# Products with v in runs of four in the second attention, and ten tiles of probabilities

## The chip, the cores and the metric

The kernel runs on one core of a Trainium2 chip. The metric is the device time of one execution in microseconds. The core has five engines with a program each, which wait for each other through semaphores: TensorE (PE in the profile, its weight loads PEld), VectorE (DVE), ScalarE (ACT), GpSimd (POOL) and SyncE (SP), which issues most DMAs here.

## The reference

Two transformer blocks on 1024 tokens of width 1024, one after the other. The first has a sliding-window attention and an MLP. The second has low-rank attention with 8 heads, a Fourier branch, a gated merge of the two, and 16 experts that pick their tokens. The change lies in the second block's attention, over 1024 latent keys and 256 context keys:

```
q, k, v = _mla_qkv(p, ...)            # q, k: 8 heads of 96; v: 8 heads of 64
qc, kc, vc = _mla_qkv(pc, ...)
k_all = concatenate([k_lat, k_ctx])   # 1280 keys
s = einsum('bqhd,bkhd->bhqk', q, k) * 96 ** -0.5
o = einsum('bhqk,bkhd->bqhd', softmax(s), v)
x = x + g1 * _merge(p, o, fourier, ...)   # then the experts
```

## The kernel before, in words

The kernel is written against a tile layer: pools of named tiles with a number of buffers each, and a scheduler that puts every engine's instructions into one fixed order when the program is built. It goes by priority (the place in the code, unless `high_priority` lifts it) and by when it reckons operands and buffers to be ready. So the code's order is not the order on the engines: an instruction that is ready early moves up into another's gap.

`attend` (L1233) goes through the 8 heads in four pairs (`main`, L1255). In a pair it takes the 10 blocks of 128 keys (`j`), and for each the two halves of 512 queries (`half`); one such (j, half) is a step, 20 in a pair. In a step, for each of the two heads (`s`):

- three fp32r passes on TensorE give the scores with keys as rows, in a PSUM bank `st` (two banks), each operand being split into a high and a low part (L1278 to L1280);
- ScalarE takes the exponential into a tile `pt` in SBUF (L1282); the negated row maximum rides along as a 97th row of the operands, so no separate subtraction is needed. `pt` has `ATT_PT` buffers, 8 before;
- the sums for the denominator are added up elementwise in `acc` (L1290, L1292), on GpSimd for the key blocks 3, 6 and 8, else on VectorE.

The products with v follow one step later: `late` holds the step, and `weigh` (L1261) issues two matmuls (L1264), one a head, in plain fp32. Each uses 64 of TensorE's columns, because a head of v is 64 wide: head 0 writes partitions 0 to 63 of the bank `av[half]`, head 1 the others. They sum over the ten key blocks; after the tenth, ScalarE copies `av` out (L1267). `finish` (L1245) sums `acc` over partitions with a matmul of ones, also 64 columns a head, takes the reciprocal on VectorE (L1251) and scales (L1253). For a pair it is issued within the next one.

Beside the steps, two pieces at a time, goes the preparation of the next pair (`att_prep`, `aside` in the code): transposes of k and q into banks `tr` (L1176), copies out of them (L1179, L1180), and the row maxima: for each head and 128 queries, score matmuls into banks `mx` (two, L1203), which VectorE reduces (L1205). In the last pair `merge_ready` takes its place and splits operands for the merge; after the last pair come merge matmuls into banks named `st`, `mx` and `mg` (`mm3`, L132 to L134), of which those with `moh` and `mol` (the halves of the last pair's result) need the last two `finish`.

PSUM has 8 banks: tr 2, mx 2, av 2, st 2.

Of the kernel before, what the change touches and what calls it, by code (L numbers as in the profile page):

```python
# [33 lines left out]
MOE_LAST = 0  # L34
MOE_FIRST = 0, 1, 2, 3
ATT_FIN = (0, 1), (1, 0)
ATT_PT, ATT_GP, ATT_ACC, ATT_TR = 8, (3, 6, 8), 1, 2
MOE_SA = 0
TOP_GROUPS = (0, 1, 2, 3), (4, 5), (6,), (7,)
POWER = (0, 2, 3)  # L40
# [75 lines left out]
class Kern:  # L116
# [1116 lines left out]
    def attend(self, pools, p, ps, O, hd, got):  # L1233


        nc = self.nc
        tr = lambda: ps.tile([128, 512], F32, name="tr", bufs=ATT_TR)
        mx = bank = None
        if ATT_TR == 1:
            mx = lambda: ps.tile([128, 1536], F32, name="mx", bufs=1)  # L1240
        else:
            bank = lambda: ps.tile([128, 512], F32, name="mx", bufs=4 - ATT_TR)
        acc = {}

        def finish(hp, half):  # L1245
            tp = tr()
            for s in range(2):
                nc.tensor.matmul(tp[s * 64:s * 64 + 64, :], lhsT=self.ones[:, :64], rhs=acc[hp, half, s], start=True, stop=True,
                                 skip_group_check=True)
            R = p.tile([128, 512], F32, name="R", bufs=2)  # L1250
            nc.vector.reciprocal(R, tp)  # L1251
            o = O[hp][:, half * 512:half * 512 + 512]
            nc.vector.tensor_mul(o, o, R)  # L1253

        def main(hp, aside):  # L1255
            heads = [hd.pop(2 * hp + s) for s in range(2)]
            av = [ps.tile([128, 512], F32, name="av", bufs=2) for _ in range(2)]
            first = {}
            late = []

            def weigh():  # L1261
                j, half, pts = late.pop(0)
                for s in range(2):
                    nc.tensor.matmul(av[half][s * 64:s * 64 + 64, :], lhsT=self.v[j][:, 2 * hp + s, :], rhs=pts[s],  # L1264
                                     start=j == 0, stop=j == 9, skip_group_check=True)
                if j == 9:
                    nc.scalar.copy(O[hp][:, half * 512:half * 512 + 512], av[half])  # L1267

            for j in range(10):
                for half in range(2):  # L1270
                    sl = slice(half * 512, half * 512 + 512)
                    pts = []
                    for s in range(2):
                        qt, kt = heads[s]
                        st = ps.tile([128, 512], F32, name="st", bufs=2)
                        ks = slice(j * 128, j * 128 + 128)
                        mm = nc.tensor.matmul
                        mm(st, lhsT=kt[0][:, ks], rhs=qt[0][:, sl], start=True, stop=False)  # L1278
                        mm(st, lhsT=kt[0][:96, ks], rhs=qt[1][:96, sl], start=False, stop=False)
                        mm(st, lhsT=kt[1][:96, ks], rhs=qt[0][:96, sl], start=False, stop=True)  # L1280
                        pt = p.tile([128, 512], F32, name="pt", bufs=ATT_PT)
                        nc.scalar.activation(pt, st, AF.Exp)  # L1282
                        pts.append(pt)
                        if j == 0:
                            first[half, s] = pt
                        else:
                            eng = nc.gpsimd if j in ATT_GP else nc.vector
                            if j == 1:
                                acc[hp, half, s] = p.tile([128, 512], F32, name=f"acc{half}{s}", bufs=ATT_ACC)
                                eng.tensor_add(acc[hp, half, s], first[half, s], pt)  # L1290
                            else:
                                eng.tensor_add(acc[hp, half, s], acc[hp, half, s], pt)  # L1292
                    late.append((j, half, pts))
                    if len(late) > 1:
                        weigh()
                    if hp and (j, half) in ATT_FIN:
                        finish(hp - 1, ATT_FIN.index((j, half)))
                    next(aside, None)
                    next(aside, None)
            weigh()  # L1300
            for _ in aside:
                pass

        for hp in range(4):
            main(hp, self.att_prep(hp + 1, pools[(hp + 1) % 2], p, hd, tr, mx, bank) if hp < 3 else
                 self.merge_ready(pools[0], O, got))

        finish(3, 0)
        for half, name in ((0, "st"), (1, "mx")):
            sl = slice(half * 512, half * 512 + 512)  # L1310
            for m in range(2):
                pt = got["pt"][m, half] = ps.tile([128, 512], F32, name=name, bufs=2)
                for k in range(3):
                    self.mm3(pt, [x[:, k, :] for x in got["w"][m]], [x[:, sl] for x in got["o"][k]], k == 0, False)
            if half == 0:
                finish(3, 1)
# [784 lines left out]
```

## Time and profile before

| | |
|---|---|
| median of 3 runs | 2281.03 us (2279.44 to 2283.23) |
| the profiled execution | 2279.89 us |
| its span, first to last instruction | 2278.1 us |
| TensorE busy, mean granted clock | 2166.4 us (95%), 0.98 |
| VectorE, ScalarE, GpSimd busy | 1775.9, 1081.7, 565.2 us |
| the second attention, first st pass to end of the last pair | 1471.5 to 1767.2 us of the span |

The busy time of TensorE is made of modelled ends: a matmul's row gives its start exactly, its duration roughly. Matmuls overlap, so the difference of two starts tells what a matmul costs in the stream. In the timeline equal instructions that follow each other are one row with a count; a fp32 matmul shows as two records (two passes), a fp32r matmul as one.

### The profile page before, as it was taken

The numbers are of one execution on the slowest core, as the hardware profiler recorded it, in microseconds if no ns is written. First come the engines' busy times: TensorE is split into PE (matmuls) and PEld (weight loads), VectorE is DVE, ScalarE is ACT, GpSimd is POOL, SyncE is SP. The second block draws the span as 40 slices with busy tenths as digits, with TensorE's granted clock in tenths as the row PEclk, the third lists the DMA queues.
The fourth block names the chain that finished last, engine by engine and source line by source line (L and its number), as shares of the span: only waits on it lengthen the run. The fifth ranks groups of instructions, "written<-read, shape, count | busy, mean of one in ns | idle before, by whom it ended". The sixth has DMA issues, their size and how long they took to land. (4 is left out here: it accounts for less than half of the span.)

```text
span 2278.1 us, 29149 instructions
## 1 busy us (share of the span) xinstructions
PE 2166.4 (95%) x9954; PEld 1628.3 (71%) x9954; DVE 1775.9 (78%) x3047; ACT 1081.7 (47%) x1976; POOL 565.2 (25%) x489
## 2 busy tenths in 40 slices
PE   8999997999998999997999999999999998599997
PEld 7667685777776888875888988744444776488886
DVE  5777888898778889999444488776775678899997
ACT  5656555333333444464443375234335243278775
POOL 2111304222122113347121025121122422421121
PEclk9999998999999999999999999999999999699999
DMA  4000223556555432202333141300000865499995
GB/s 152 28 20 11 111 92 122 176 185 214 210 182 198 148 133 81 83 38 74 118 109 114 61 170 47 137 1 10 10 1 10 305 225 199 156 377 386 385 386 153
DMA packets 94965, 319.87 MB, mean 140 GB/s; under 512 B 13568, under 2 KB 15424, under 8 KB 94816
## 3 DMA queue, kind: packets, MB, share of 16 engines
q1 hardware_dynamic: 89856, 300.10, 36.0%
q0 software_dynamic: 4816, 17.39, 3.0%
q8 instruction: 78, 1.28, 0.2%
q14 instruction: 71, 0.58, 0.1%
q10 hardware_dynamic: 144, 0.52, 0.1%
HBM read 259.13 MB, written 58.75 MB: 140 GB/s over the span
## 5 line engine op out<-in xcount | busy, mean ns | idle before, releaser
L127 ACT CAST we_hi<-we_raw 128x1024 fp32r<-128x1024 f32 x192 | 200.1, 1051 | 60.5 <-PE gu L134 40.9
L128 DVE TENSOR_TENSOR we_lo<-we_raw,we_hi 128x1024 fp32r<-128x1024 f32 x188 | 222.1, 1222 | 3.7 <-ACT we_hi L127 3.4
L127 ACT CAST wup_h<-raw 128x512 fp32r<-128x512 f32 x154 | 94.9, 621 | 245.6 <-PE A L133 136.4
L128 DVE TENSOR_TENSOR wup_l<-raw,wup_h 128x512 fp32r<-128x512 f32 x154 | 122.6, 804 | 87.0 <-ACT wup_h L127 84.4
L1282 ACT ACTIVATE pt<-st 128x512 f32<-128x512 f32 x160 | 95.2, 596 | 134.9 <-PE st L1280 123.7
L132 PE MATMUL A<-uh,wup_h 128*128 128x512 f32 x364 | 146.9, 404 | 4.1 <-ACT a_raw L528 2.1
L133 PE MATMUL A<-ul,wup_h 128*128 128x512 f32 x364 | 146.2, 402 | 3.5 <-DVE ul L128 3.4
L134 PE MATMUL A<-uh,wup_l 128*128 128x512 f32 x364 | 145.2, 400 | 2.4 <-DVE wup_l L128 2.3
L127 ACT CAST dah<-a_raw 128x512 fp32r<-128x512 f32 x92 | 57.4, 623 | 139.5 <-PE B L133 67.5
L1264 PE MATMUL av<-pt,v 128*64 128x512 f32 x320 | 119.5, 616 | 0.0
L1292 POOL TENSOR_TENSOR acc<-acc,pt 128x512 f32<-128x512 f32 x48 | 65.3, 1375 | 211.8 <-ACT pt L1282 115.7
L441 POOL TENSOR_TENSOR wup_s<-raw 128x512 f32<-128x512 f32 x24 | 33.7, 1403 | 332.1 <-DVE raw L440 330.2
L1205 DVE TENSOR_REDUCE nm<-mx 128x1 f32<-128x512 f32 (+1 forms) x120 | 79.9, 687 | 43.9 <-PE mx L1203 42.8
L133 PE MATMUL B<-dwl,dah 128*128 128x512 f32 x272 | 107.5, 395 | 2.7 <-DVE dwl L128 2.6
L132 PE MATMUL B<-dwh,dah 128*128 128x512 f32 x272 | 107.2, 397 | 1.7 <-ACT dwh L127 1.7
L134 PE MATMUL B<-dwh,dal 128*128 128x512 f32 x272 | 106.8, 393 | 0.3 <-DVE dal L128 0.3
L133 PE MATMUL A<-dwl,dah 128*128 128x512 f32 x256 | 102.3, 400 | 4.4 <-DVE dwl L128 4.4
L132 PE MATMUL gu<-we_hi,xh 128*128 128x512 f32 x256 | 105.0, 410 | 0.0
L455 POOL TENSOR_TENSOR a_raw<-a_raw,a_raw 128x512 f32<-128x512 f32 x16 | 52.0, 3252 | 211.4 <-DVE a_raw L440 194.5
L132 PE MATMUL A<-dwh,dah 128*128 128x512 f32 x256 | 101.2, 398 | 2.7 <-ACT x_sq L812 2.7
L133 PE MATMUL gu<-we_lo,xh 128*128 128x512 f32 x256 | 102.0, 399 | 0.0
L134 PE MATMUL gu<-we_hi,xl 128*128 128x512 f32 x256 | 101.5, 396 | 0.0
(692 smaller groups left out, 6448.9 us busy)
## 6 DMA issues: line engine op xcount, KB each, us to landing
we_raw<-in_w_eg SPq DMA_DIRECT2D x64, 512.0 KB
we_raw<-in_w_eu SPq DMA_DIRECT2D x64, 512.0 KB
we_raw<-in_w_ed SPq DMA_DIRECT2D x64, 512.0 KB
h<-in_w_mod SPq DMA_DIRECT2D x48, 512.0 KB
raw<-in_w_up SPq DMA_DIRECT2D x32, 512.0 KB
ad<-r_out SPq DMA_DIRECT2D x32, 512.0 KB
a_raw<-ad SPq DMA_DIRECT2D x32, 512.0 KB
w_raw<-in_w_dn SPq DMA_DIRECT2D x32, 512.0 KB
```

What stands on the lines that cost most here:

```text
L127: pin(self.nc.scalar.copy(hi, raw))
L128: pin((eng or self.nc.vector).tensor_sub(lo, raw, hi.bitcast(F32)))
L132: mm(ps, lhsT=l[0], rhs=r[0], start=start, stop=False, **kw)
L133: mm(ps, lhsT=l[0], rhs=r[1], start=False, stop=False, **kw)
L134: mm(ps, lhsT=l[1], rhs=r[0], start=False, stop=stop, **kw)
L441: e[1].tensor_sub(t, x[3], x[0])
L455: e[3].tensor_add(x[2], x[2], x[3])
L1205: most = lambda o, i: nc.vector.tensor_reduce(o, i, axis=AX.X, op=OP.max, negate=True)
L1264: nc.tensor.matmul(av[half][s * 64:s * 64 + 64, :], lhsT=self.v[j][:, 2 * hp + s, :], rhs=pts[s], start=j == 0, stop=j == 9, skip_group_ch ...
L1282: nc.scalar.activation(pt, st, AF.Exp)
L1292: eng.tensor_add(acc[hp, half, s], acc[hp, half, s], pt)
```

## The change

`weigh` is called when two steps are held, ahead of the third, and issues the four products of both steps in a row. All but the first of the four have high priority and are kept in program order, which binds them to the first in the scheduler's order. The copies out follow the whole run. `ATT_PT` goes from 8 to 10.

```diff
-ATT_PT, ATT_GP, ATT_ACC, ATT_TR = 8, (3, 6, 8), 1, 2
+ATT_PT, ATT_GP, ATT_ACC, ATT_TR = 10, (3, 6, 8), 1, 2
...
+            def weigh():
+
+                ends = []
+                for n, (j, half, pts) in enumerate(late):
+                    for s in range(2):
+                        with self.tc.high_priority() if n + s else ExitStack():
+                            mm = nc.tensor.matmul(av[half][s * 64:s * 64 + 64, :], lhsT=self.v[j][:, 2 * hp + s, :], rhs=pts[s],
+                                                  start=j == 0, stop=j == 9, skip_group_check=True)
+                            if n + s:
+                                self.tc.keep_in_program_order(mm)
+                    if j == 9:
+                        ends.append(half)
+                late.clear()
+                for half in ends:
+                    nc.scalar.copy(O[hp][:, half * 512:half * 512 + 512], av[half])
+
             late = []
-
-            def weigh():
-                j, half, pts = late.pop(0)
-                for s in range(2):
-                    nc.tensor.matmul(av[half][s * 64:s * 64 + 64, :], lhsT=self.v[j][:, 2 * hp + s, :], rhs=pts[s],
-                                     start=j == 0, stop=j == 9, skip_group_check=True)
-                if j == 9:
-                    nc.scalar.copy(O[hp][:, half * 512:half * 512 + 512], av[half])
-
...
+                    if len(late) == 2:
+                        weigh()
                     late.append((j, half, pts))
-                    if len(late) > 1:
-                        weigh()
```

What it makes of the order on the engines, at three places. First TensorE in the first pair, key block 3 (`v_11879`), before:

```order
L1264 MATMUL av<-pt,v_11879 64x512
L1203 MATMUL mx<-kth,qth 128x512 x2
L1264 MATMUL av<-pt,v_11879 64x512
L1278 MATMUL st<-qth,kth 128x512
L1279 MATMUL st<-qtl,kth 128x512
L1280 MATMUL st<-qth,ktl 128x512
L1203 MATMUL mx<-kth,qth 128x512
L1278 MATMUL st<-qth,kth 128x512
L1279 MATMUL st<-qtl,kth 128x512
L1203 MATMUL mx<-kth,qth 128x256 x2
L1280 MATMUL st<-qth,ktl 128x512
L1264 MATMUL av<-pt,v_11879 64x512
```

and the same key block after (st is at L1286 to L1288 there, av at L1266):

```order
L1203 MATMUL mx<-kth,qth 128x512
L1286 MATMUL st<-qth,kth 128x512
L1287 MATMUL st<-qtl,kth 128x512
L1203 MATMUL mx<-kth,qth 128x512
L1288 MATMUL st<-qth,ktl 128x512
L1266 MATMUL av<-pt,v_11879 64x512 x4
L1203 MATMUL mx<-kth,qth 128x512
L1203 MATMUL mx<-kth,qth 128x256 x2
```

Before, mx matmuls stand between the two heads of a step; after, the four products of the key block follow each other.

Second, TensorE at the end of the last pair (`v_11884` is key block 8, the merge matmul of L133 writes an mx bank), before:

```order
L1278 MATMUL st<-qth,kth 128x512
L1279 MATMUL st<-qtl,kth 128x512
L1280 MATMUL st<-qth,ktl 128x512
L1264 MATMUL av<-pt,v_11884 64x512 x2
L1278 MATMUL st<-qth,kth 128x512
L1279 MATMUL st<-qtl,kth 128x512
L1280 MATMUL st<-qth,ktl 128x512
L1278 MATMUL st<-qth,kth 128x512
L1279 MATMUL st<-qtl,kth 128x512
L1280 MATMUL st<-qth,ktl 128x512
L1264 MATMUL av<-pt,v_11885 64x512 x4
```

and after:

```order
L1286 MATMUL st<-qth,kth 128x512
L1287 MATMUL st<-qtl,kth 128x512
L1288 MATMUL st<-qth,ktl 128x512
L133 MATMUL mx<-qtl,ktl 128x512
L1286 MATMUL st<-qth,kth 128x512
L1287 MATMUL st<-qtl,kth 128x512
L1288 MATMUL st<-qth,ktl 128x512
L1286 MATMUL st<-qth,kth 128x512
L1287 MATMUL st<-qtl,kth 128x512
L1288 MATMUL st<-qth,ktl 128x512
L1266 MATMUL av<-pt,v_11885 64x512 x4
```

Here heads already stood together; what moved is a merge matmul, which came from behind the last product.

Third, VectorE in the first pair (reductions of mx at L1205, adds at L1292), before:

```order
L1205 TENSOR_REDUCE nm_13247<-mx 128x1 x2
L1205 TENSOR_REDUCE nm_13247<-mx 128x2
L1292 TENSOR_TENSOR acc_13190<-acc_13190,pt 128x512
L1205 TENSOR_REDUCE nm_13247<-mx 128x1 x4
L1292 TENSOR_TENSOR acc_13198<-acc_13198,pt 128x512
L1205 TENSOR_REDUCE nm_13247<-mx 128x2
L1205 TENSOR_REDUCE nm_13247<-mx 128x1 x2
```

and after (adds at L1300):

```order
L1205 TENSOR_REDUCE nm_13245<-mx 128x1
L1300 TENSOR_TENSOR acc_13188<-acc_13188,pt 128x512
L1300 TENSOR_TENSOR acc_13196<-acc_13196,pt 128x512
L1205 TENSOR_REDUCE nm_13245<-mx 128x1
L1205 TENSOR_REDUCE nm_13245<-mx 128x2
L1205 TENSOR_REDUCE nm_13245<-mx 128x1 x4
L1205 TENSOR_REDUCE nm_13245<-mx 128x2
L1205 TENSOR_REDUCE nm_13245<-mx 128x1 x2
```

The two adds stood among the reductions; after, they stand together, ahead of nine of them.

## Rows read from the trace of the kernel before

**Rows 1.** The page: busy time, share of the span, instructions of each engine.
```profile
PE 2166.4 (95%) x9954; PEld 1628.3 (71%) x9954; DVE 1775.9 (78%) x3047; ACT 1081.7 (47%) x1976; POOL 565.2 (25%) x489
```

**Rows 2.** Windows, the four pairs: length, PE, PEld, DVE, ACT, POOL, clock, DMA share, GB/s.
```profile
1471.54:1549.84 78.30, 77.35 (x287) 38.45 (x286) 52.19 (x79) 31.97 (x54) 20.77 (x16) 1.00 0.02 8
1549.84:1629.23 79.39, 79.01 (x296) 38.99 (x294) 57.42 (x82) 31.23 (x54) 16.52 (x12) 1.00 0.02 7
1629.23:1711.36 82.13, 82.03 (x297) 39.26 (x295) 58.31 (x84) 31.97 (x57) 16.20 (x12) 1.00 0.02 7
1711.36:1767.17 55.81, 55.81 (x211) 26.33 (x211) 31.24 (x36) 28.30 (x50) 16.31 (x12) 1.00 0.04 14
```

**Rows 3.** The same view, 250 us of the experts.
```profile
2000.00:2250.00 250.00, 250.00 (x1163) 203.58 (x1162) 244.37 (x250) 199.60 (x222) 47.17 (x26) 1.00 1.00 371
```

**Rows 4.** Line 1264: count, duration ns min/median/max, first and last start, forms.
```profile
L1264 PEld LDWEIGHTS av<-pt,v x320: 132/135/138, 1476.0 to 1766.3; 128*64 128x64 f32 x160
L1264 PE MATMUL av<-pt,v x320: 592/593/645, 1476.0 to 1766.7; 128*64 128x512 f32 x160
```

**Rows 5.** Timeline of TensorE: start, duration, line, tiles, columns, count.
```profile
1512.16 1.08 PE L1264 MATMUL av<-pt,v 128*64 128x512 f32 x4
1513.17 0.50 PE L1278 MATMUL st<-qth,kth 97*128 97x512 f32 x1
...
1514.77 1.07 PE L1264 MATMUL av<-pt,v 128*64 128x512 f32 x2
1515.77 0.74 PE L1203 MATMUL mx<-kth,qth 96*128 96x256 f32 x3
```

**Rows 6.** Timeline of TensorE, a run of four before a st pass.
```profile
1709.49 1.94 PE L1264 MATMUL av<-pt,v 128*64 128x512 f32 x8
1711.36 0.50 PE L1278 MATMUL st<-qth,kth 97*128 97x512 f32 x1
1711.70 0.40 PE L1279 MATMUL st<-qtl,kth 96*128 96x512 f32 x1
1711.93 0.40 PE L1280 MATMUL st<-qth,ktl 96*128 96x512 f32 x1
```

**Rows 7.** Timeline of TensorE, one step of the last pair.
```profile
1728.59 0.39 PE L1280 MATMUL st<-qth,ktl 96*128 96x512 f32 x1
1728.91 1.08 PE L1264 MATMUL av<-pt,v 128*64 128x512 f32 x4
...
1731.52 1.08 PE L1264 MATMUL av<-pt,v 128*64 128x512 f32 x4
```

**Rows 8.** Timeline behind the last product; in brackets idle time before and releaser.
```profile
1773.60 3.36 DVE L1251 RECIPROCAL R<-tr 128x512 f32<-128x512 f32 x1 [0.83 <-PE tr L1248]
...
1776.87 0.63 DVE L128 TENSOR_TENSOR mol<-o,moh 128x512 fp32r<-128x512 f32 x1
...
1777.90 0.39 PE L133 MATMUL st<-mol,kth 128*128 128x512 f32 x1
```

**Rows 9.** Windows 1486.7:1537.9, 1571.6:1623.6, 1651.9:1703.9, their sum and mean.
```profile
sum 155.20, PE 155.10 PEld 74.95 DVE 111.30 ACT 48.87 POOL 38.65; mean PE 51.70 PEld 24.98 DVE 37.10 ACT 16.29 POOL 12.88
```

**Rows 10.** VectorE's groups in 1542.5:1624: busy, mean ns, idle before.
```profile
L1205 DVE TENSOR_REDUCE nm<-mx 128x1 f32<-128x512 f32 (+1 forms) x40 | 26.6, 688 | 14.2 <-PE mx L1203 13.6
...
L1251 DVE RECIPROCAL R<-tr 128x512 f32<-128x512 f32 x2 | 6.7, 3351 | 1.7 <-PE tr L1248 1.7
```

**Rows 11.** Waits in 1471:1768: who for whom, us in total, times, longest.
```profile
DVE nm L1205 <- PE mx L1203: 42.8, 44, 1.7
...
PEld mx L1203 <- DVE nm L1205: 15.6, 21, 0.8
...
ACT pt L1282 <- POOL acc L1292: 2.8, 1, 2.8
```

**Rows 12.** Timeline, the last pass of a st and its exponential.
```profile
1522.52 0.40 PE L1280 MATMUL st<-qth,ktl 96*128 96x512 f32 x1
...
1522.95 0.60 ACT L1282 ACTIVATE pt<-st 128x512 f32<-128x512 f32 x1 [3.21 <-PE st L1280]
```

## The prediction

> **What bounds the kernel now.** I read the page's busy shares first, then the attention stage cut into its four pairs of heads, then TensorE's own timeline inside a pair. TensorE is busy 95% of the span [rows 1], and in the second attention it has hardly a gap: 294 of 296 us, at a granted clock of 1.00, that is 2.4 GHz, while VectorE is busy 31 to 58 us in a pair of 56 to 82 us [rows 2]. So what ends the stage is the sum of what TensorE executes, and the change is worth what it takes out of that sum, as long as no other engine becomes late. Behind the stage nothing is tied to an absolute time: DMA moves 0.02 to 0.04 of its share while the pairs run [rows 2], the expert weights are loaded afterwards, and in the experts TensorE is busy 250.0 us of 250 [rows 3]. Time saved here should arrive at the end whole.
>
> Busy times hide the point, because the ends of matmuls are modelled; I use the distance from one start to the next. An ordinary 512-column pass takes 0.23 us (1711.70 to 1711.93 [rows 6]). The products with v are fp32: 160 instructions give 320 passes on 64 columns [rows 4], two passes each. After one head alone the next instruction starts 1.00 later (1514.77 to 1515.77). After two heads next to each other, which lie on different halves of the 128 columns, it starts 1.01 later (1512.16 to 1513.17 [rows 5]): the second head is free. A run of four before a st pass takes 1.87 (1709.49 to 1711.36), and the first st pass behind any run takes 0.34 instead of 0.23 (1711.36 to 1711.70 [rows 6]). The last st pass ahead of a run takes 0.32 (1728.59 to 1728.91 [rows 7]).
>
> That gives two prices. A further pair inside a run costs 1.87 - 1.01 = 0.86 us (a "unit": one head, or two on opposite halves). Entering and leaving costs once a run 0.09 + (1.01 - 0.86) + 0.11 = 0.35, a little less beside other passes than st; I take 0.34. Check: a step of the last pair is six st passes, one run, one unit: 1.40 + 0.34 + 0.86 = 2.60; measured 2.61 (1728.91 to 1731.52 [rows 7]).
>
> **The change part by part.** *Runs.* Counted in TensorE's order over the stage, with the eight pairs of denominator sums (finish), which use the same half width: before 112 runs with 122 units (64 products stand alone, 40 times two, 4 times four); after 50 runs with 92 units (36 of four products, the rest one to three). Before: 112 x 0.34 + 122 x 0.86 = 143.0. After: 50 x 0.34 + 92 x 0.86 = 96.1. Saved: 46.9 us. With 0.23 for each other full pass, TensorE's sum of the pairs goes from 76.9, 78.6, 81.3, 55.7 (the trace has 78.3, 79.4, 82.1, 55.8 [rows 2]) to 63.8, 63.4, 66.5, 54.4. Nearly all lies in the first three pairs, where the row maxima (mx) stood between the heads of a pair; in the last one only every second entry goes.
>
> The Trainium skill, "TensorE: Matmul & The Clock Gate", section "The mechanism", speaks against runs of four: a weight load overlaps matmuls in flight only when the row group differs, and all these products use all the rows. By that rule the later loads, 0.133 us each, would stand bare, a run of four would take about 2.27, and some 14 us of the gain would go. The rows show such loads at 0.13 us [rows 4] and yet 1.87 for the eight passes [rows 6], so the trace contradicts it here and I keep 1.87.
>
> *The last pair's fillers and the tail.* Eleven of the 18 merge passes into mx that stood behind the last product now stand between the st passes of the last pair. There they cost 11 x 0.23 = 2.6. In the tail they leave a hole: the passes with mol need the second reciprocal (1773.60, 3.36 long) and then mol (from 1776.87, 0.63); TensorE comes there just in time today (1777.90 [rows 8]). It will come 2.6 earlier and wait. VectorE's order there also puts both gate products ahead of the second mol, so the first mg pass comes some 0.6 later, counted from the last product. Cost 3.2; bounds 0 (the hole fills) and 5.
>
> *VectorE beside the mx passes.* This cover may fail. In the three stretches with mx VectorE is busy 37.1 us of 51.7 [rows 9], with 40 reductions of 0.69 in each [rows 10]. TensorE's sum for such a stretch falls to 40.1, 40.3 and 42.2, mean 40.9, and VectorE gets two more adds into it (14 or 15, not 12 or 13): 37.1 + 2 x 0.69 = 38.5, which is 94%, with two banks of mx between the two. Two steps (four st, some six mx banks, a run of four) are about 6.3 us on TensorE; VectorE needs 6 x 0.69 = 4.1 and, where the adds are its own, 4 x 0.69 = 2.8: 0.6 too long. For three of nine key blocks GpSimd adds, and VectorE has 2 us to spare. Some four periods a pair overrun, and part of it flows into the free ones, since during a run of four VectorE can catch up for 1.87 us. I take 2 us a pair. Bounds: below, -1 a pair, if today's waits go too (the first three pairs are 1.4, 0.8 and 0.8 over their sums); above, VectorE keeps its share of 37.1/51.7 = 0.72 and a stretch takes 38.5/0.72 = 53.5, 12.6 over TensorE's sum. I stay near the low end because the overrun is small and the adds may lag.
>
> *Pair starts.* A reciprocal holds VectorE 3.35 us, twice a pair [rows 10], while tr has two banks. The starts shrink from 26.6 to 23.1 us by the same sums; 0.8 a pair, 2.5 in all, bounds 0 and 6.
>
> *Ten pt tiles.* Up to six are held for the products (four before), so four remain for the adds, as now. The exponentials wait 2.8 us in all for GpSimd's adds [rows 11]; cost nothing, since the same four cover them. What it costs without that cover is the third rival.
>
> *Exponentials.* One starts 0.43 after the start of the last pass of its st and takes 0.60 [rows 12]. With two st banks, four st in a row would wait 0.1 to 0.2 us; the order has mx or merge passes between them nearly everywhere, so nothing.
>
> Sum: -46.9 + 3.2 + 6 + 2.5 = -35.2. The profiled execution took 2279.9, which gives 2244.7; the median of the runs is 1.1 above it, so 2246.
>
> **The rivals.** *VectorE sets the pace of the mx stretches.* For it: 94% on one side, 100% on the other, strict order on both. Against: its reductions wait for TensorE today far more than the other way round (42.8 us against 15.6 [rows 11]). Halfway between the shares, at 0.83, a stretch takes 46.4, 5.5 over TensorE's sum, 16.5 in all: gain 46.9 - 3.2 - 16.5 - 2.5 = 25, so 2256. At the bound 38 stands for 16.5: gain 3, 2277.
>
> *Everything is hidden.* No new wait in the stretches or at the starts: -46.9 + 3.2 = -43.7, so 2237; without the tail's loss 2234.
>
> *Slower: the pt ring stops TensorE.* The products give back four tiles at once and late. If the adds lag by more than the four spare tiles, the next exponential waits for a whole run, and the st passes behind it wait for that exponential. Price: 0.43 + 0.60, a restart of 0.11 and half a microsecond of lag, some 1.6 us in each of the 40 periods of two steps: 64 us, so 2236 + 64 + 1 = 2301. It decides from 1.1 us a period on. Against: 2.8 us of such waits in the whole stage [rows 11], with as many spare tiles.
>
> *A run of four costs more than 1.87.* For it only that four runs stand in the trace, not 36; 0.4 more in each takes 14 us: 2260. By the rule of the Trainium skill weighed above it would come to the same.
>
> **How the numbers follow.** Forecast (2240 to 2252) 60%; hidden 13%; VectorE's pace 19%, a tenth of it at its bound; a dearer run 2%; pt ring 4%; no visible change, by whatever adds up, 2%. The range 2236 to 2263 leaves out the pt ring, the far end of VectorE's pace, no change, and a third of "hidden". 0.2% is 4.6 us, about what a measurement of this kernel tells from no change: faster 0.94, same 0.03, slower 0.03.
>
> **What would show it.** Right: in the profile after, products in rows of x8 with 1.87 to the next start, some 36 of them; the first three pairs 65 to 69 us long, the last 54 to 55; VectorE at 85 to 95% in the mx stretches; a wait of 2 us ahead of the first mol pass. Wrong: mx passes that start half a microsecond late all along (VectorE's pace), exponentials that wait for adds (the ring), or a run of four longer than 1.9.

## The result, and the profile after

The changed kernel takes 2246.62 us in the median of four runs (2245.16 to 2249.41), the kernel before 2281.05 beside it: a ratio of 0.9854, 95% interval 0.9841 to 0.9866. The forecast was 2246, faster. Its profiled execution took 2246.17 us, with a span of 2244.4 in place of 2278.1.

The same windows as in [rows 2], the four pairs of the changed kernel (length; busy time of PE, PEld, DVE, ACT, POOL; clock; DMA share; GB/s), and their sum:

```profile
1471.76:1538.58 66.82, 66.01 (x292) 38.63 (x290) 52.56 (x79) 32.29 (x55) 21.92 (x16) 1.00 0.03 9
1538.58:1605.14 66.56, 65.67 (x292) 37.25 (x291) 60.10 (x82) 30.54 (x53) 16.73 (x12) 1.00 0.03 9
1605.14:1674.90 69.76, 68.35 (x296) 38.96 (x294) 60.26 (x84) 31.88 (x56) 16.62 (x12) 1.00 0.03 9
1674.90:1730.57 55.67, 55.67 (x222) 29.23 (x222) 28.51 (x37) 28.55 (x51) 14.98 (x12) 1.00 0.04 13
sum 258.81, PE 255.70 PEld 144.08 DVE 201.43 ACT 123.27 POOL 70.25; mean PE 63.92 PEld 36.02 DVE 50.36 ACT 30.82 POOL 17.56
```

The four pairs take 258.8 us in place of 295.6, so 36.8 less; VectorE works about as long as before in them (201.4 us, 199.2 before), in a shorter time. TensorE's sum by the two prices of the prediction is 248.1: the pairs stand 3.0, 3.2, 3.3 and 1.3 us over it, 10.7 in all (3.1 before).

TensorE's timeline, a run of four between a st and an mx pass, answers to [rows 6]:

```profile
1497.60 0.39 PE L1288 MATMUL st<-qth,ktl 96*128 96x512 f32 x1
1497.92 1.94 PE L1266 MATMUL av<-pt,v 128*64 128x512 f32 x8
1499.79 0.50 PE L1203 MATMUL mx<-kth,qth 96*128 96x512 f32 x1
```

The last pass ahead of the run takes 0.32 and the run 1.87, as before. There are 36 such rows of x8: 34 take 1.87 to the next start, one 1.77 and one 2.21.

The three stretches with mx passes (called the stretches from here on), answering to [rows 9] (same columns as the pairs):

```profile
1487.20:1528.70 41.50, 41.06 (x183) 24.85 (x181) 38.04 (x60) 17.01 (x29) 13.56 (x10) 1.00 0.00 1
1558.30:1601.30 43.00, 42.11 (x181) 24.62 (x180) 41.98 (x60) 17.66 (x30) 16.73 (x12) 1.00 0.00 1
1626.90:1671.30 44.40, 42.99 (x186) 25.95 (x186) 41.32 (x59) 18.28 (x31) 16.62 (x12) 1.00 0.00 1
sum 128.90, PE 126.16 PEld 75.42 DVE 121.34 ACT 52.95 POOL 46.92; mean PE 42.05 PEld 25.14 DVE 40.45 ACT 17.65 POOL 15.64
```

VectorE is busy 94% of them, 72% before. TensorE's own sums are 40.1, 40.3 and 42.2, so before rounding they stand 6.2 over in all (0.3 before).

The waits of the four pairs, answering to [rows 11] (who for whom, us, times, longest):

```profile
PEld mx L1203 <- DVE acc L1300: 9.7, 12, 0.8
PEld mx L1203 <- DVE nm L1205: 8.7, 19, 1.3
DVE nm L1205 <- PE mx L1203: 7.4, 11, 1.9
...
PE mx L1203 <- DVE nm L1205: 2.6, 6, 0.9
```

The reductions waited 42.8 us for TensorE before, now 7.4; and TensorE's matmuls themselves, not only its weight loads, wait for a reduction.

The tail, answering to [rows 8]: the rows of TensorE ahead of the first pass with mol, and of the first gate product (mg) and the experts' first matmul (gu):

```profile
1738.81 0.39 PE L132 MATMUL st<-moh,ktl 128*128 128x512 f32 x1
1740.96 0.50 PE L133 MATMUL st<-mol,kth 128*128 128x512 f32 x1 [1.76 <-DVE mol L128]
...
1744.43 0.50 PE L133 MATMUL mx<-mol,kth 128*128 128x512 f32 x1 [1.48 <-DVE mol L128]
...
1745.46 0.39 PE L132 MATMUL mg<-qth,wm_hi 128*128 128x512 f32 x1
...
1932.61 0.79 PE L132 MATMUL gu<-we_hi,xh 128*128 128x512 f32 x1
```

From the end of the last pair to mg it is 14.9 us (13.8 before), to gu 202.0 (200.5 before).

### The profile page after: what moved, and what is told of

It reads as the page before. It is cut to its first block, busy times and chain, and to the rows that moved or that the text cites. A ratio compares the mean times of both kernels' runs of the same rounds, so it can differ in the third digit from the quotient of the medians.

```text
span 2244.4 us, 29157 instructions
## 1 busy us (share of the span) xinstructions
PE 2126.8 (95%) x9954; PEld 1628.1 (73%) x9954; DVE 1778.0 (79%) x3047; ACT 1081.9 (48%) x1976; POOL 566.2 (25%) x489
## 3 DMA queue, kind: packets, MB, share of 16 engines
q8 instruction: 78, 1.28, 0.2%
## 5 line engine op out<-in xcount | busy, mean ns | idle before, releaser
L133 PE MATMUL A<-ul,wup_h 128*128 128x512 f32 x364 | 145.8, 401 | 3.5 <-DVE ul L128 3.4
L133 PE MATMUL B<-dwl,dah 128*128 128x512 f32 x272 | 107.6, 396 | 2.8 <-DVE dwl L128 2.7
L1300 POOL TENSOR_TENSOR acc<-acc,pt 128x512 f32<-128x512 f32 x48 | 64.5, 1361 | 176.0 <-ACT pt L1290 139.3
L133 PE MATMUL A<-dwl,dah 128*128 128x512 f32 x256 | 102.0, 398 | 4.3 <-DVE dwl L128 4.3
L133 PE MATMUL gu<-we_lo,xh 128*128 128x512 f32 x256 | 101.9, 398 | 0.0
L134 PE MATMUL A<-dwh,dal 128*128 128x512 f32 x256 | 101.0, 394 | 0.0
L133 PE MATMUL B<-ul,wup_h 128*128 128x512 f32 x228 | 91.6, 402 | 7.8 <-POOL ul L128 4.0
```

The source lines that it names most:

```text
L133: mm(ps, lhsT=l[0], rhs=r[1], start=False, stop=False, **kw)
L134: mm(ps, lhsT=l[1], rhs=r[0], start=False, stop=stop, **kw)
```

## Experiments

Each median below has the kernel before beside it on the same chip (2279.60 to 2280.81); every account of pairs, stretches and tail is read from one profiled execution of a kernel. "Over the sum" means longer than TensorE's sum by the two prices. Three theories were on trial. A: that sum alone decides. B: VectorE's load in the stretches is a second bound. C, which came up on the way: single VectorE adds stand still while GpSimd adds.

**The tiles.** First the kernel before with ten tiles alone, then the changed kernel with eight.

```diff
-ATT_PT, ATT_GP, ATT_ACC, ATT_TR = 8, (3, 6, 8), 1, 2
+ATT_PT, ATT_GP, ATT_ACC, ATT_TR = 10, (3, 6, 8), 1, 2
```

> The kernel before with ten tiles of probabilities and nothing else; TensorE's order has the same 112 runs and 122 units. Theory (what TensorE executes sets the time: 0.34 us a run of half-width products, 0.86 a unit): no change, 2279 to 2283. Rival (the tiles: the exponentials were held up by eight tiles, and the two more give a good part of the 34 us): 2250 to 2270.

```diff
-ATT_PT, ATT_GP, ATT_ACC, ATT_TR = 10, (3, 6, 8), 1, 2
+ATT_PT, ATT_GP, ATT_ACC, ATT_TR = 8, (3, 6, 8), 1, 2
```

> The kernel after with eight tiles of probabilities; TensorE's order has the same runs and units. Six tiles are held for the products, so two are left for the adds instead of four. Theory: the order on TensorE decides, and the adds run close behind: 2246 to 2251. Rival (the ring of tiles stops TensorE as soon as the adds lag by more than two tiles): 0.5 us and more in each of 40 periods, 2266 or above.

2281.0 (ratio 1.0002, 0.9993 to 1.0012) and 2248.36 (0.9854, 0.9838 to 0.9871); the pairs take 295.5 and 259.1. The tiles do nothing by themselves and aren't needed: the ring of tiles as a slower outcome is out.

**Delay without binding.** The four products are still issued together, but not bound to each other:

```diff
-                        with self.tc.high_priority() if n + s else ExitStack():
...
-                            if n + s:
-                                self.tc.keep_in_program_order(mm)
```

> The kernel after without priority and without kept order for the products: they still wait for two steps, but the scheduler may put other passes between them: 86 runs with 122 units. Theory: 26 runs at 0.34 are saved and no unit, 8.8 us, less some waits: 2271 to 2277. Rival (the longer wait before the products is what helps, since TensorE never waits for an exponential): 2246 to 2255.

2271.41 (0.9962, 0.9948 to 0.9976). Its order has 86 runs and 122 units, so TensorE's sum is 283.7; the pairs take 286.5. The two prices hold at a third mix of runs and units, and the rival, that waiting longer before the products is what helps, is out.

**Binding without delay.** Only the two heads of a step stand together:

```diff
-                    if len(late) == 2:
+                    if len(late) == 1:
```

> The kernel after, but the products go one step late as before, so that only the two heads of a step are bound together: 81 runs with 91 units (before 112 and 122, after 50 and 92). Theory: TensorE's sum over the pairs is 255.3 us (before 292.5, after 248.1); with some 7 us of waits, and the merge passes still in the tail, 2247 to 2252. Rival (the gain comes from the switches between half and full width alone, 34 us for 62 runs, 0.55 us each): 31 runs fewer give 17 us, 2264.

2246.37 (0.985, 0.9834 to 0.9867), just under what was expected: the whole gain, with 81 runs and 91 units, nearly every run of one unit. TensorE's sum is 255.3, 7.2 more than in the changed kernel, yet the pairs take 260.6, only 1.8 more. The sum of its three stretches with mx:

```profile
sum 123.60, PE 123.50 PEld 69.80 DVE 110.31 ACT 48.71 POOL 38.68; mean PE 41.17 PEld 23.27 DVE 36.77 ACT 16.24 POOL 12.89
```

They stand 1.5 us over TensorE's own 122.1; in the changed kernel it was 6.2. So what the runs of four save comes back: 4.7 as waits there, 0.7 elsewhere in the pairs, and 1.7 behind them (gu at 200.3 after the last pair, not 202.0). So theory A falls, and the gain doesn't need the runs of four. The rival on record, 2264, is out as well.

**VectorE heavier and lighter.** All adds on VectorE; then four key blocks on GpSimd, with runs of four and without.

```diff
-ATT_PT, ATT_GP, ATT_ACC, ATT_TR = 10, (3, 6, 8), 1, 2
+ATT_PT, ATT_GP, ATT_ACC, ATT_TR = 10, (), 1, 2
```

> The changed kernel, but VectorE does all ten key blocks' adds: 12 adds of 0.69 us, 8.3 us, more for it in each pair. TensorE's sum by the two prices (62 runs, 104 units in its order, since the last pair's products fall apart) is 61.8, 67.8, 66.9, 66.1 = 262.6 us, 14.5 more than in the changed kernel. Theory, VectorE is as much the bound of the first three pairs as TensorE: its 53 to 60 us a pair become 61 to 68, as long as TensorE's own sum, and the first three pairs take 5 or more over that sum each; about 283 us in all, so 2265 to 2273 us. Rival, TensorE's sum decides and the changed kernel's 10.7 us over it are a fixed loss: 273 us, so 2261 us.

```diff
-ATT_PT, ATT_GP, ATT_ACC, ATT_TR = 10, (3, 6, 8), 1, 2
+ATT_PT, ATT_GP, ATT_ACC, ATT_TR = 10, (2, 4, 6, 8), 1, 2
```

> The changed kernel, but GpSimd adds four key blocks (2, 4, 6, 8) in place of three: VectorE has 4 adds of 0.69 us, 2.8 us, less in each pair, GpSimd four more. TensorE's sum (47 runs, 89 units) is 61.9, 64.1, 64.2, 53.6 = 243.8 us, 4.3 less. Theory: VectorE gets lighter by 2.8 and TensorE by 1.9 to 2.3 in the first and third pair, so the waits shrink a little: pairs about 252 to 254 us for 258.8, so 2239 to 2243 us. Rival, GpSimd becomes late (its adds take twice VectorE's time) and the exponentials wait for it: 2246 us or more.

The same, without runs of four:

```diff
-ATT_PT, ATT_GP, ATT_ACC, ATT_TR = 10, (3, 6, 8), 1, 2
+ATT_PT, ATT_GP, ATT_ACC, ATT_TR = 10, (2, 4, 6, 8), 1, 2
...
-                    if len(late) == 2:
+                    if len(late) == 1:
```

> Only the two heads of a step stand together (no runs of four), with GpSimd adding the key blocks 2, 4, 6, 8. TensorE's sum (78 runs, 89 units) is 64.9, 66.6, 66.6, 54.5 = 252.6 us, 8.8 more than that of the kernel with runs of four and the same four key blocks. Theory, what fewer runs save on TensorE is given back as waits for VectorE: it ends within 3 us of that kernel, 2240 to 2246 us. Rival, with a lighter VectorE the runs of four bring their 31 x 0.34 us: it ends 7 to 9 us behind it, about 2250 us.

They took 2259.07 (0.9911, 0.9894 to 0.9927), 2244.29 (0.9847, 0.983 to 0.9863) and 2247.36 (0.9856, 0.9839 to 0.9872). Theory B failed on the first two. With 12 more adds a pair on VectorE, the pairs take 272.3, 9.7 over TensorE's sum and not 20, near the rival, and the stretches only 1.4 over theirs. With 4 adds fewer a pair, the pairs stand 12.9 over the sum, more than in the changed kernel, and the stretches 8.3. The third ends 3.1 us behind the second, where B had at most 3 and its rival 7 to 9.

In two of these traces something else has a part: TensorE's granted clock. With all adds on VectorE, TensorE waits 1.6 us in the third pair for VectorE's adds, and shortly after the clock is 0.50 (1.2 GHz) for 3.4 us; the third kernel has a wait of 2.1 and the same fall in its first pair. The 3.4 us at half clock do the work of 1.7 at 1.00, so some 1.7 of the 9.7 is the clock's, and as much of the 5.4 us that the third kernel's pairs take more than the second's.

What went the wrong way shows in the groups of adds in the third stretch (busy, mean ns). The changed kernel first, VectorE's and GpSimd's:

```profile
L1300 POOL TENSOR_TENSOR acc<-acc,pt 128x512 f32<-128x512 f32 x12 | 16.6, 1401 | 52.9 <-ACT pt L1290 34.9 <-DVE acc L1300 17.3 <-DVE nm L1224 0.8
L1300 DVE TENSOR_TENSOR acc<-acc,pt 128x512 f32<-128x512 f32 x15 | 14.0, 973 | 0.0
```

The kernel before, and the one with two heads together:

```profile
L1292 DVE TENSOR_TENSOR acc<-acc,pt 128x512 f32<-128x512 f32 x14 | 10.9, 793 | 0.0
L1300 DVE TENSOR_TENSOR acc<-acc,pt 128x512 f32<-128x512 f32 x14 | 11.1, 805 | 0.0
```

All adds on VectorE:

```profile
L1300 DVE TENSOR_TENSOR acc<-acc,pt 128x512 f32<-128x512 f32 x19 | 12.3, 681 | 0.0
```

Four key blocks on GpSimd:

```profile
L1300 DVE TENSOR_TENSOR acc<-acc,pt 128x512 f32<-128x512 f32 x12 | 11.8, 1017 | 0.0
```

Nineteen adds alone take less than fifteen beside GpSimd, and hardly more than twelve. The changed kernel's timeline of the place, VectorE, GpSimd and the mx passes:

```profile
1653.29 4.11 DVE L1300 TENSOR_TENSOR acc<-acc,pt 128x512 f32<-128x512 f32 x3
1655.24 3.27 POOL L1300 TENSOR_TENSOR acc<-acc,pt 128x512 f32<-128x512 f32 x2 [0.70 <-DVE acc L1300]
1655.25 0.73 PE L1203 MATMUL mx<-kth,qth 96*128 96x512 f32 x2
1657.32 3.36 DVE L1205 TENSOR_REDUCE nm<-mx 128x1 f32<-128x512 f32 x5
1658.05 0.50 PE L1203 MATMUL mx<-kth,qth 96*128 96x512 f32 x1 [0.91 <-DVE nm L1205]
```

Three adds take 4.11 us in place of 2.05 while GpSimd adds at the same time; the reductions behind them come late, both mx banks are full, and TensorE waits 0.91. Over the whole attention, VectorE's adds that touch none of GpSimd's take 0.67 to 0.69, those beside one up to 1.82. All fourteen that take over 0.7 start while a GpSimd instruction runs and end 0.55 us behind one, two of them behind instructions that write `raw` and share no tile with the adds; so it isn't a wait for data. That is theory C. The Trainium skill states it: by "SBUF — State Buffer", section "Who interferes with whom", a VectorE instruction with two inputs in SBUF contends with a GpSimd instruction that reads SBUF; the ports that they share are an exclusive lock, and issue order decides who blocks. This trace agrees for the adds; the reductions, with one input from PSUM, keep their 0.69 beside GpSimd.

Added up over the three stretches, VectorE's adds lose 3.0 us this way before, 3.1 with two heads together, 9.7 in the changed kernel, 10.1 with four key blocks on GpSimd, and nothing where VectorE does them all. The waits over TensorE's sum go the same way: 0.3, 1.5, 6.2, 8.3, but 1.4 for the last.

**Fewer adds on VectorE, GpSimd's kept.** These kernels leave the adds of five key blocks out. With runs of four, then with two heads, where `len(late) == 1` stands again in the place of `len(late) == 2`:

```diff
-                        else:
+                        elif j == 1 or j in ATT_GP:
...
-                                eng.tensor_add(acc[hp, half, s], first[half, s], pt)
+                                eng.scalar_tensor_tensor(acc[hp, half, s], first[half, s], 1.0, pt, op0=OP.add, op1=OP.add)
```

> The changed kernel without VectorE's adds for the key blocks 2, 4, 5, 7 and 9 (left out of the denominators; a constant keeps them positive): VectorE has 20 adds of 0.69 us, 13.8 us, less in each pair, and nothing else is taken away. TensorE's sum by its order (51 runs, 92 units) is 65.1, 63.4, 65.3, 54.4 = 248.2 us, that of the changed kernel (248.1). Theory, the waits of the changed kernel's pairs (10.7 us over the sum) are waits for VectorE: they fall to 3 to 5 us, the pairs take 251 to 253 us, and the time is 2239 to 2242 us. Rival, they belong to the runs of four themselves (a loss at each run that the two prices miss): the pairs stay at 257 us or more.

> The same adds left out, with only the two heads of a step together (no runs of four). TensorE's sum (78 runs, 89 units) is 64.9, 66.6, 66.6, 54.5 = 252.6 us, 4.4 more than that of the kernel with runs of four and the same adds. Theory: with VectorE lightened both stand 3 to 5 us over their sums, so the pairs take 255 to 258 us and runs of four now bring 3 to 5 us in the pairs, which they did not with all the adds (1.8 us of 7.2). Rival, the waits have another cause: this kernel stands 5 over its sum as with all the adds, and the one with runs of four 10 over, so it is the shorter one of the two by a microsecond or more.

2240.68 (0.9825, 0.981 to 0.984) and 2244.2 (0.9839, 0.9824 to 0.9854). The pairs with runs of four take 252.9, 4.7 over the sum, and the stretches 1.6 over, as expected. Those with two heads take 261.0, 8.4 over the sum where 3 to 5 were expected; their stretches are 2.5 over. Most of the rest lies right behind the stretches of the second and third pair: in both TensorE waits 1.4 to 1.5 us for VectorE's last step on the row maxima (`nm`, L1224), and in the second the granted clock then falls:

```profile
1601.70:1604.90 3.20, 3.20 (x8) 1.32 (x5) 0.00 (x0) 0.53 (x1) 2.46 (x2) 0.50 0.01 1
```

That is 1.2 GHz for 3.4 us, some 1.7 lost. So of the 8.1 us that the runs of four bring in the pairs here, TensorE's sums account for 4.4. Runs of four do pay on TensorE once VectorE's adds are out of the way. Since these kernels take away the load and the meetings with GpSimd together, they don't tell B from C; the last experiment does.

**The tail.** The second `finish(3, 1)` right behind the first:

```diff
         finish(3, 0)
+        finish(3, 1)
...
-            if half == 0:
-                finish(3, 1)
```

> The changed kernel, but in the tail the second finish of the last pair stands in the code right behind the first, ahead of the first half's merge products. The order of the pairs on TensorE stays. Theory, the hole in the tail is VectorE's order, both gate products ahead of the second mol: with the second reciprocal and mol earlier the tail shrinks from 14.9 us to 12.5 to 13.5, the pairs stay at 258 to 260, and the time is 2244 to 2246 us. Rival, the tail is bound by the two reciprocals of 3.4 us whatever the order: the tail stays at 14.5 or more, 2246 to 2247 us.

2245.48 (0.9846, 0.983 to 0.9863), within the scatter of the changed kernel. The tail did shrink, to 12.0, and the first mg pass comes 2.9 us earlier behind the last pair; but gu still starts 201.9 behind it. Followed pass by pass, the lead goes at two places. Some 47 us behind the last pair, TensorE waits 1.2 and 0.9 us for operands of the merge (`mh`, `ml`; the changed kernel waits 0.7 once), and then its granted clock is 0.50, where it stays at 1.00 in the changed kernel:

```profile
1781.60:1784.80 3.20, 3.20 (x8) 2.47 (x8) 3.20 (x10) 1.64 (x4) 0.84 (x1) 0.50 0.97 333
```

Behind this place 0.9 of the 2.9 us are left: the waits took 1.2 and the slower clock, after some catching up, 0.8. The last 0.9 goes at the reload of x, in VectorE's timeline:

```profile
1812.15 1.29 DVE L1493 TENSOR_TENSOR x<-x,x3t 128x512 f32<-128x512 f32 x2 [2.92 <-DMA x<-x2d]
```

In this order SyncE issues that reload 74.3 us behind the last pair, the changed kernel 69.6. Whether the reload would have swallowed the whole lead at full clock isn't shown.

**A better version.** Runs of four in the first three pairs only, four key blocks on GpSimd (against the changed kernel):

```diff
-ATT_PT, ATT_GP, ATT_ACC, ATT_TR = 10, (3, 6, 8), 1, 2
+ATT_PT, ATT_GP, ATT_ACC, ATT_TR = 10, (2, 4, 6, 8), 1, 2
...
-                    if len(late) == 2:
+                    if len(late) == (2 if hp < 3 else 1):
```

> Runs of four in the first three pairs only, one step at a time in the last, and GpSimd adding the key blocks 2, 4, 6, 8. TensorE's order of the first three pairs is that of the kernel with these four key blocks and runs of four throughout (61.9, 64.1, 64.2); in the last pair no merge pass moves in between (54.5 for 53.6). Theory, moving the merge passes into the last pair costs 1.7 us up to the experts' first matmul (202.0 us from the pair's end for 200.3): pairs 257, experts' first matmul 200.3 us behind them, 2241 to 2244 us in all. Rival, the 1.7 us belong to other differences in the order behind the pairs and stay: 2244 to 2245 us.

2242.65 (2241.9 to 2243.59; 0.9835, 0.9822 to 0.9849); pairs 256.9, gu 200.4 behind them. Against the kernel with these four key blocks and runs of four throughout, gu comes 1.6 us earlier behind the last pair, and the last pair itself takes only 0.2 longer.

Then theory C put to use, starting from that kernel: in the first three pairs GpSimd adds one early key block, and VectorE all that fall into the stretches.

```diff
-ATT_PT, ATT_GP, ATT_ACC, ATT_TR = 10, (2, 4, 6, 8), 1, 2
+ATT_PT, ATT_GP, ATT_ACC, ATT_TR = 10, ((1,), (1,), (1,), (2, 4, 6, 8)), 1, 2
...
-                            eng = nc.gpsimd if j in ATT_GP else nc.vector
+                            eng = nc.gpsimd if j in ATT_GP[hp] else nc.vector
```

> Runs of four in the first three pairs, one step at a time in the last; GpSimd adds only the key block 1 in the first three pairs (ahead of the stretches with mx) and the blocks 2, 4, 6, 8 in the last. VectorE so has 18 or 19 adds in each mx stretch, 3 or 4 more than in the changed kernel. TensorE's sum by its order is 61.8, 65.4, 65.4, 54.8 = 247.4 us, its sum of the mx stretches 41.8, 41.6, 41.6. Theory, the waits in the mx stretches come from VectorE's adds that stand still while GpSimd adds (1.07 to 1.82 us in place of 0.69 in the changed kernel's trace), more than from their number: without GpSimd there VectorE's adds take 0.69 each, the stretches stay within 0.8 us of their sums (1.3 to 2.7 in the changed kernel), the pairs take 252 to 255 us, and the time is 2238 to 2241 us. Rival, VectorE's number of operations decides: with 3 or 4 more adds a stretch (2.1 to 2.8 us) the stretches stand 2 to 4 us over their sums, the pairs take 257 us or more, and the time is 2243 us or more.

2237.7 (2234.49 to 2239.98; 0.9812, 0.9798 to 0.9825): faster than all kernels above that compute the whole result, with an interval below the changed kernel's. The pairs take 252.3, 4.9 over the sum, though VectorE has more adds in the stretches than in the changed kernel; B had 257 or more. Its three stretches, POOL being the last busy time:

```profile
1487.70:1531.60 43.90, 42.47 (x188) 26.27 (x187) 40.57 (x64) 18.05 (x30) 0.97 (x2) 1.00 0.00 1
1556.00:1597.90 41.90, 41.90 (x187) 26.54 (x186) 38.70 (x62) 18.03 (x30) 0.00 (x0) 1.00 0.00 1
1622.00:1663.80 41.80, 41.80 (x186) 26.55 (x186) 38.65 (x62) 18.03 (x30) 0.00 (x0) 1.00 0.00 1
```

The second and third stand 0.2 us over TensorE's 41.6, with VectorE at 92%. The first is 2.2 over its 41.8, against the 0.8 that was expected, and its timeline has one wait for nearly all of that:

```profile
1485.44 1.30 POOL L1168 TENSOR_TENSOR raw<-kn,kr 128x640 f32<-128x640 f32 x1
1485.94 3.88 DVE L1300 TENSOR_TENSOR acc<-acc,pt 128x512 f32<-128x512 f32 x2
1486.68 1.28 POOL L1298 TENSOR_TENSOR acc<-pt 128x512 f32<-128x512 f32 x1
...
1487.90 0.76 POOL L1169 TENSOR_TENSOR raw<-kp,kr 128x320 f32<-128x320 f32 x1
1489.74 0.68 DVE L1205 TENSOR_REDUCE nm<-mx 128x1 f32<-128x512 f32 x1
...
1490.48 0.39 PE L1203 MATMUL mx<-kth,qth 96*128 96x256 f32 x1 [1.43 <-DVE nm L1205]
```

Two adds take 3.88 us behind three instructions of GpSimd, and TensorE waits 1.43 for the reduction that follows. So the one stretch that still waits is the one at whose start GpSimd still runs.

## Why the prediction was right, point by point

*Runs, 46.9 saved.* The prices held: 1.87 for 34 of the 36 runs, and the unbound kernel 2.8 us over its sum. The sentence of the Trainium skill that spoke against runs of four ("TensorE: Matmul & The Clock Gate", section "The mechanism": a load overlaps matmuls in flight only when the row group differs) stays contradicted, since bare loads would have made 2.27. The same section also lets a load into the background weight buffer run ahead of matmuls in flight; the prediction left that out, and it would fit the 1.87, though no run here shows which buffer a load goes to. What the prediction did not see is that its parts differ in worth: putting a pair's heads together gives all of the net gain, and the second step in a run nothing, since its 7.2 us on TensorE come back as waits.

*VectorE beside the mx passes, 6.* Measured 6.2 less 0.3, so 5.9. The size was right and the cause half wrong. I worked it out from VectorE's load, with every add at 0.69 us. Load alone is not it: at 92%, with 18 or 19 adds and none on GpSimd, a stretch waits 0.2 us; in the changed kernel, with 15 adds and 10 to 12 of GpSimd's beside them, the stretches wait 1.3 at 92% and 2.2 and 2.7 at 93 and 98%. The waits follow the adds that GpSimd blocks. Nor do the shorter stretches alone bring these meetings: with two heads together they are as short, with 9 to 10 adds of GpSimd, and VectorE's adds lose no more than before (3.1 and 3.0 us). It is the order with runs of four in which they lose 9.7; what in it brings the adds together wasn't tried.

*Pair starts, 2.5.* Outside the stretches, the waits grew from 2.8 to 4.5 in all four pairs, 1.2 of these 1.7 us in the last one. For the starts this leaves 0.5, within the bounds of 0 and 6 but a fifth of the size.

*The last pair's fillers and the tail, 3.2.* The 2.6 are in TensorE's sum. The two waits for mol came as foreseen (1.76 and 1.48), and mg starts 1.1 later, not 0.6. Further on a little more is lost: gu starts 1.5 later, and the order of the merge differs there too. Moving the reciprocal forward gave nothing back at gu.

*Tiles and exponentials, nothing.* For the tiles confirmed from both sides, with ten tiles alone and with eight. For the exponentials, no matmul of TensorE is seen to wait for one in the pairs; its weight loads do, for 5.4 us in all ahead of st passes (28.0 before) and 6.7 ahead of products (0.8 before).

*Sum.* The pairs give 36.8, the tail up to gu takes 1.5 back, the experts 1.0: from first to last gu 287.8 us in place of 286.7. The 1.0 is the clock's, which the prediction had at nothing. Three of the fourteen kernels show 287.8, the changed one, the one with four key blocks and two heads, and the one with runs of four in three pairs; the others show 286.5 to 286.7 over the same program. In the traces of these three alone, and in that order here, TensorE's granted clock falls to 0.50 some 16 to 17 us behind the first gu; the last line is the same place in the kernel before:

```profile
1949.40:1952.60 3.20, 3.20 (x14) 2.71 (x12) 2.83 (x4) 1.45 (x2) 0.00 (x0) 0.50 0.36 131
1951.00:1954.30 3.30, 3.30 (x11) 2.61 (x11) 2.86 (x3) 0.33 (x1) 0.00 (x0) 0.50 0.44 154
1945.80:1949.00 3.20, 3.20 (x13) 2.76 (x12) 2.94 (x4) 1.53 (x2) 0.00 (x0) 0.50 0.30 111
1984.00:1991.00 7.00, 7.00 (x36) 5.76 (x35) 6.91 (x8) 4.58 (x6) 0.00 (x0) 1.00 0.63 148
```

TensorE waited 1.07 us for GpSimd shortly before, but so it did in the kernels whose clock stays at 1.00; why it falls in some isn't shown, nor whether it does in every execution of a kernel. A later start and end take 0.6, and 33.7 arrive of 35.2. That the median met the forecast to within a microsecond owes something to luck: runs scatter by 4 us, and two misses cancel in part, waits in the pairs 0.9 us under the forecast, and 2.5 us more than forecast elsewhere.

## What to carry to other kernels

Work out what a reordering saves on the bound engine, then ask for each of its parts alone whether the engine beside it can follow: here the simpler half (two heads together) gave everything, and the second half paid only once VectorE was freed. Moving work to a slower helper engine can cost more than it relieves where the two engines' instructions meet and block each other: look at the durations of equal instructions with and without the helper beside them, not at the busy share alone. A hole closed in a chain is worth something only if nothing further along it waits for something else, here operands of the merge and a reload. And before a leftover microsecond is called scatter or put down to an order, look at the granted clock of the stretch that it lies in.

## What the runs showed of the hardware

An add of 128x512 f32 with both inputs in SBUF takes VectorE 0.67 to 0.69 us alone and up to 1.82 beside a GpSimd add of 1.28; when it starts during a GpSimd instruction and is held up, it ends 0.55 us behind that one. A reduction from PSUM is unmoved at 0.69. In the changed kernel a GpSimd add that starts during one of VectorE's takes 1.60 to 1.73. Products of 64 columns with eight weight loads of 0.135 us in a row took 1.87 us a run, 34 times of 36. And between the first pair and the last gu, seven of the fourteen traces have one or two stretches of 3.4 us in which TensorE's granted clock is 0.50, besides the longer one around the first gu that all have; each begins within 2 us behind a wait of TensorE of 0.9 to 2.1 us, while waits as long stand elsewhere without a fall.
